# Four numbers of a recording kernel's time estimate set anew: split product, GpSimd step, two DRAM transfers

## The chip, the cores and the metric

The kernel runs on one core of a Trainium2 chip. The metric is the device time of one execution in microseconds (us). Three runs of the kernel before gave 1656.69, 1654.39 and 1648.88 us, with a median of 1654.39 us.

## The reference, cut to what matters

Two layers act on 256 tokens of width 1024. Each layer is a feed-forward block, a mixer with three branches, and a second feed-forward block, each added to the stream after a root-mean-square norm:

```python
for l in range(DEPTH):                       # DEPTH = 2
    x = x + 0.5 * swiglu(rms_norm(x, ffn1_norm[l]), ffn1_w_gate[l], ffn1_w_up[l], ffn1_w_down[l])
    x = x + hybrid_mixer(rms_norm(x, mix_norm[l]), w_in[l], ...)
    x = x + 0.5 * swiglu(rms_norm(x, ffn2_norm[l]), ffn2_w_gate[l], ffn2_w_up[l], ffn2_w_down[l])

# inside the mixer, on proj = u @ w_in:
ya = rg_lru(conv(rg_x), ...) * gelu(rg_gate)                       # branch 0
yb = softmax-weighted dilated attention, 12 heads in 3 groups      # branch 1
yc = rms_norm(chunk_gated_delta_rule(q, k, v, g, beta)) * silu(z)  # branch 2, 8 heads
y  = (gate0 * (ya @ wa) + gate1 * (yb @ wb) + gate2 * (yc @ wc)) @ w_out

# inside the delta rule: the inverse of a unit lower triangular matrix
sol = triangular_solve(a + eye(C), concat([vb, kb * exp(gam)]), lower=True, unit_diagonal=True)
```

## The kernel before, in words

**Products.** Every weight matrix is read once from DRAM, in chunks of up to 1024 columns of 128 rows (tile `raw`). A chunk is split into a high part `wh` (a copy, mostly on ScalarE) and a low part `wl` (raw minus high, on VectorE). The activations are split in the same way into pairs of tiles `s`. One step of the inner dimension is then three matmuls of 128x128 weights on 256 columns into a PSUM bank `big`: high by high, high by low, low by high. A chunk of 1024 columns holds eight steps, that is 24 such split products. There are 12144 of them in the program, and TensorE (PE) does little else: the other matmuls, into banks `sm`, belong to attention, the delta rule and the norms. Five chunks can stand converted at once (NCONV) and six raw (NRAW).

**Order.** The order of each engine's instructions is fixed when the program is written out, by a recording layer. The split products are issued one after another in a fixed sequence of jobs. All other work is written as generators ("tasks"). After each split product `pump` looks which tasks are due and lets them issue their next few instructions. A task is due when the estimated end of what it issued last has passed on the estimated clock of PE. The estimates come from `Engine._cost` (lines 327 to 368), plus a lag per engine, and `cur.t` is moved on by hand after a DMA. On the chip each engine then works through its own list in that order, and waits by semaphores: an instruction whose data is late holds up everything behind it on its engine.

**The delta rule.** Task `pair` (from line 1033) treats two heads; there are four pairs in each layer, so eight in all. Its triangular inverse goes like this. VectorE writes the diagonal 16x16 blocks to `A16` (line 1121; on the engine it reads `TENSOR_TENSOR arena<-arena 128x64`). A DMA writes them to DRAM (`rd`, line 1123), a second one reads them back, spread over all partitions, into `RR`, 1024 columns of the arena (line 1127). GpSimd (POOL) then does 30 small steps (lines 1137 to 1141), which invert the blocks, and only then is `RR` given back (line 1143). VectorE spreads the result with one multiply into `M32` (line 1149; `TENSOR_TENSOR arena<-arena,cst 128x128`), transposes it, and PE goes on with 16x16 and 32x32 products (`MATMUL sm<-arena 32x16`), then 64x64 and 128x128 ones.

**Attention.** Task `heads4` treats four heads (two slots of two). For each slot it takes twice 1152 columns of the arena, multiplies queries by keys, adds the distance term on VectorE (`SCALAR_TENSOR_TENSOR arena<-cst,sm 128x384`), takes a maximum, the exponential and the sum, scales, transposes on PE and multiplies by the values. While pairs are unfinished, tasks without an order number, such as `heads4`, may take arena space only if 3072 columns stay free (`keep`). The products of branch 1 need its results `yb`, those of branch 2 need `yc`.

The lines that the change touches are 336, 358, 1124 and 1130:

```python
336                return max(0.427 * n, 0.83 * m)
358            return (330 + 160 * n) if k.get("op") == ALU.pow else 240 + 2.2 * n
1124        self.cur.t += 2200.0
1130        self.cur.t += 2800.0
```

Of the kernel before, what the change touches and what calls it, by code (L numbers as in the profile page):

```python
# [13 lines left out]
ALU = mybir.AluOpType  # L14
# [6 lines left out]
T = 256  # L21
# [224 lines left out]


class Slots:
    """Places of T columns, each taken by one tile after another, of either type."""

    def __init__(self, pr, pool, n):
        self.pr, self.pool = pr, pool
# [52 lines left out]
def _free(ap):  # L305
    n = 1
    for x in ap.shape[1:]:
        n *= x
    return n


class Engine:
    """An engine whose instructions are counted into the estimate of the time that the order is chosen by."""

    def __init__(self, pr, key, eng):
        self._pr, self._key, self._eng = pr, key, eng
# [12 lines left out]
    def _cost(self, name, a, k):  # L329
        key = self._key  # L330
        if key == "pe":
            lhsT = k["lhsT"] if name == "matmul" else a[1]
            rhs = k["rhs"] if name == "matmul" else a[2]
            n, m = _free(rhs), _free(lhsT)
            if lhsT.dtype == F32R:
                return max(0.427 * n, 0.83 * m)
            if name == "transpose":
                return 0.84 * max(n, m)
            if m <= 32 and lhsT.shape[0] <= 32:
                return 40.0  # L340
            if m <= 64 and lhsT.shape[0] <= 64 and n <= 64:
                return 100.0
            return 1.7 * max(n, m)
        n = _free(a[0])
        if name == "tensor_reduce":
            n = _free(a[1])
        if key == "a":
            c = 93 + 0.833 * n
            for x in ("scale", "bias", "accum_out"):
                c += 93 * (not isinstance(k.get(x, 0.0), float) and x in k)  # L350
            func = a[2] if name == "activation" else None
            sets = TABLES.get(func)
            if sets and self._pr.table not in sets:
                self._pr.table = sets[0]
                c += 1283
            return c
        if key == "g":
            return (330 + 160 * n) if k.get("op") == ALU.pow else 240 + 2.2 * n
        if name == "reciprocal":
            return 68 + 6.3 * n  # L360
        fast = name in ("tensor_copy", "tensor_scalar") and a[1].space != PSUM
        c = 68 + (0.52 if fast else 1.04) * n
        if name in ("scalar_tensor_tensor", "tensor_scalar") and not isinstance(a[2], float):
            c += 60
        if k.get("accum_out") is not None:
            c += 60
        return c
# [5 lines left out]
class Prog:  # L373
# [65 lines left out]
        o += l * PRM["_n"]  # L439
        return self.prm[:, o:o + n]  # L440

# [1 line left out]
    @property  # L443
    def now(self):
        return self.clock["pe"]
# [132 lines left out]
        assert None not in out  # L578
        return out

# [1 line left out]
    def load_group(self, part=None):  # L582
        gi = self.dma_next
        self.dma_next += 1
        for key in [x for x in self.raw_t if x[0] == gi - NRAW]:
            del self.raw_t[key]
        cols = self.groups[gi][1]
        src = self.io["wts"][self.goff[gi]:self.goff[gi] + P * cols].rearrange("(p c) -> p c", p=P)
        if part is not None:
            n = cols // 2  # L590
            s = slice(part * n, part * n + n)
            self.dma_next -= 1 - part
        else:
            s = slice(0, cols)
        self.raw_t[gi, s.stop] = self.load(self.raw[gi % NRAW][:, s], src[:, s])
# [40 lines left out]
        c = next(s.stop for s in self.pieces(k) if s.stop > col)  # L636
        self.until(lambda: self.conv_t.get((k, c), 1e18) <= self.now)

# [1 line left out]
    def need(self, *key):  # L640
        self.until(lambda: self.when.get(key, 1e18) <= self.now)
        h, l = self.ops[key]
        return h.ap, l.ap
# [49 lines left out]
                    if k < total:  # L693
                        self.pump()

# [1 line left out]
    def refresh(self, j, gain, start=False):  # L697
        xj = self.X[:, j, :]
        hl = yield from self.halves()
        self.move(hl[0].ap, xj, gain[:, j:j + 1])  # L700
        yield
        self.v.scalar_tensor_tensor(hl[1].ap, xj, gain[:, j:j + 1], hl[0].ap.bitcast(F32), op0=ALU.mult, op1=ALU.subtract)
        self.mark("x", j, hl)
        if start:
            self.cur.rank = 2
            yield
        if self.nsq is None:
            self.nsq = 0
            self.a.activation(self.ssq, xj, AF.Square)
        else:  # L710
            sq = yield from self.space(T)
            self.a.activation(sq.ap, xj, AF.Square)
            yield
            self.v.tensor_tensor(self.ssq, self.ssq, sq.ap, op=ALU.add)
            sq.free()
        yield
        self.nsq += 1
# [20 lines left out]
        sq.free()  # L738
        self.norm_ready = True

# [1 line left out]
    def ffn(self, l, w, next_gain, last):  # L742
        self.norm_ready = False
        self.spawn(self.norm_chain(), 1)
        jobs = ffn_jobs(l, w)
        for kind, f, chunks in jobs[:KF]:
            b = self.big_bank()
            for i, ch in enumerate(chunks):
                self.stationary(b[:, i * T:(i + 1) * T], [ch], "x", done=f == KF - 1 and i == 1)
            self.spawn(self.gate_up(b, f), 1)  # L750
        for kind, j, chunks in jobs[KF:]:
            b = self.big_bank()
            self.stationary(b[:, :T], chunks, "h", done=j == KD - 1)
            self.spawn(self.residual(b, 0.5, j, next_gain, last), 1)
# [23 lines left out]
        else:  # L778
            yield from self.refresh(j, next_gain)

# [1 line left out]
    def move(self, dst, src, scale=None):  # L782
        """A copy, times a constant or a column, by the engine that will be through with it first."""
        n, now = _free(src), self.now
        ap = scale is not None and not isinstance(scale, float)
        ta = max(self.clock["a"], now) + 93 + 0.833 * n + 93 * ap
        tv = max(self.clock["v"], now) + 68 + (1.04 if src.space == PSUM else 0.52) * n + 60 * ap
        step = self.step
        self.step = set()
        if ta <= tv + TILT:  # L790
            self.a.activation(dst, src, AF.Copy, **({} if scale is None else {"scale": scale}))
        elif scale is None:
            self.v.tensor_copy(dst, src)
        else:
            self.v.tensor_scalar(dst, src, scale, None, op0=ALU.mult)
        self.step = step | {"m"}
# [52 lines left out]
        self.v.tensor_tensor(hl[1].ap, src, hl[0].ap.bitcast(F32), op=ALU.subtract)  # L849
        self.mark(key, k, hl)  # L850

# [1 line left out]
    def prepare(self, l):  # L853
        lam = self.p(l, "lam")
        z, = self.tinies(1, 8)
        self.v.tensor_scalar(z.ap, lam, -1.0, None, op0=ALU.mult)
        yield
        yield from self.softplus_tiny(self.rc[l][:, 0:8], z.ap, -8.0)
        yield
        self.v.tensor_scalar(self.rc[l][:, 8:16], self.rc[l][:, 0:8], -1.0, None, op0=ALU.mult)  # L860
        self.v.tensor_scalar(self.qg[l].ap, self.p(l, "qn"), 0.125, None, op0=ALU.mult)
        z.free()
        yield EXP
        self.a.activation(self.ea[l].ap, self.p(l, "alog"), AF.Exp)
        self.prepared.add(l)
# [162 lines left out]
    def pair(self, l, h0):  # L1028
# [36 lines left out]
        A, QT = yield from self.spaces([512, 1024])  # L1065
# [3 lines left out]
        for hh, h in enumerate(heads):  # L1069
# [8 lines left out]
            n = 2 * hh  # L1078
# [42 lines left out]
        self.v.tensor_tensor(a16, t4[:, :, 0, :], t4[:, :, 1, :], op=ALU.add)  # L1121
        yield
        self.nc.sync.dma_start(self.rdram[l][h0 // 2], A16.ap)
        self.cur.t += 2200.0
        yield
        src = self.rdram[l][h0 // 2].rearrange("(b k) c -> b (k c)", k=16)
        self.nc.sync.dma_start(RR.ap, src.unsqueeze(1).to_broadcast([8, 16, 1024]))
        t1.free()
        A16.free()
        self.cur.t += 2800.0  # L1130
        yield
        r4 = RR.v("p (k n j) -> p n k j", n=4, k=16)
        M16, tmp = yield from self.spaces([64, 64])
# [138 lines left out]
        for hh in range(2):  # L1272
            n = 2 * hh + 1
# [59 lines left out]
            for x in (self.beta, self.gam, self.suf):  # L1333
                x.free()

# [1 line left out]
    def att_v(self, b, g):  # L1337
        v = yield from self.space(2 * T)
        self.move(v.ap, b)
        self.big.give(b)  # L1340
        yield
        self.vt[g] = v
# [106 lines left out]
                for x in d.values():  # L1449
                    x.free()  # L1450

# [1 line left out]
    def conv_rg(self, b, l, j):  # L1453
        y = yield from self.space(T)
        w = self.p(l, "rgw")[:, 4 * j:4 * j + 4]
        s = b[:, :T]
        self.a.activation(y.ap, s, AF.Identity, scale=w[:, 3:4], bias=self.p(l, "rgb")[:, j:j + 1])
        yield
        for k in (1, 2, 3):
            self.v.scalar_tensor_tensor(y[:, k:], s[:, :T - k], w[:, 3 - k:4 - k], y[:, k:], op0=ALU.mult, op1=ALU.add)  # L1460
            if k < 3:
                yield
        self.big.give(b)
        yield
        self.xa[j] = y
# [65 lines left out]
            yield  # L1531
            self.hr[j] = self.xa[j]

# [1 line left out]
    def merge(self, b, i):  # L1535
        t = yield from self.space(T)
        self.a.activation(t.ap, b[:, :T], AF.Tanh, scale=0.5)
        self.big.give(b)
        yield
        self.tg[i] = t  # L1540
# [164 lines left out]
```

## Time and profile before

| | |
|---|---|
| median of three runs (lowest, highest) | 1654.39 us (1648.88, 1656.69) |
| profiled execution: span from first to last instruction | 1649.0 us |
| PE busy | 1611.5 us (98%) |
| VectorE (DVE) busy | 1147.7 us (70%) |
| ScalarE (ACT) busy | 932.1 us (57%) |
| GpSimd (POOL) busy | 127.3 us (8%) |
| chain that ended last | PE, products into `big` |

The page gives the span alone for the profiled execution; the lowest of the three runs, 1648.88 us, is its nearest neighbour. PE is never far from full, so what can be read off is small: where PE stands still and for whom, and where it runs at a lower granted clock. Both happen only in the two mixers, from about 300 to 550 us and from about 1100 to 1350 us. In the rows below, line L323 is the recording layer itself, through which all instructions go; the tile names tell the work apart.

### The profile page before, as it was taken

What the parts mean: (1) busy time and instruction counts of PE and PEld (TensorE: products, weight loads), DVE (VectorE), ACT (ScalarE), POOL (GpSimd) and SP (SyncE); (2) the same over time, 40 slices, a digit from 0 to 9 for tenths busy, and PEclk for the clock granted to TensorE, in tenths of its full rate; (3) what the DMA queues carried; (4) which work ended last, traced back from release to release, by engine and by line L of the source; (5) the groups of instructions that cost most, each with busy time, mean ns of one, the idle gap of its engine ahead of it and who ended that gap; (6) DMA issues with size and microseconds to landing.
All of it is one profiled execution on the core that took longest, in us unless ns stands there. A gap on an engine that the chain in (4) does not pass through costs nothing. (4 is left out here: it accounts for less than half of the span.)

```text
span 1649.0 us, 34412 instructions
## 1 busy us (share of the span) xinstructions
PE 1611.5 (98%) x13952; PEld 1569.5 (95%) x13952; DVE 1147.7 (70%) x2156; ACT 932.1 (57%) x1652; POOL 127.3 (8%) x280
## 2 busy tenths in 40 slices
PE   9999999899999999999999999998989999999999
PEld 8999999888888999999999999998989989999999
DVE  8665688777875667666566656887868746676653
ACT  6544456776855546444454445667768545464442
POOL 0000000235102000000000000002440020000000
PEclk9999999998999999999999999999999999999999
DMA  8655655444243555555655555654533435665552
GB/s 309 185 186 181 189 191 187 136 141 137 95 154 106 182 190 185 187 189 173 196 185 190 179 184 184 193 180 128 168 110 122 143 111 174 193 188 183 185 184 89
DMA packets 84943, 279.05 MB, mean 169 GB/s; under 512 B 10256, under 2 KB 15664, under 8 KB 84784
## 3 DMA queue, kind: packets, MB, share of 16 engines
q1 hardware_dynamic: 84784, 276.85, 53.6%
q8 instruction: 110, 1.80, 0.4%
q14 instruction: 49, 0.40, 0.1%
HBM read 275.49 MB, written 1.33 MB: 168 GB/s over the span
## 5 line engine op out<-in xcount | busy, mean ns | idle before, releaser
L323 PE MATMUL big<-s,wh 128*128 128x256 f32 (+1 forms) x7520 | 1354.2, 281 | 4.1 <-DVE s L323 1.9
L323 PEld LDWEIGHTS big<-s,wh 128*128 128x128 f32 (+1 forms) x7520 | 1154.8, 188 | 15.4 <-issue 6.3
L323 PE MATMUL big<-s,wl 128*128 128x256 f32 (+1 forms) x3760 | 1057.0, 281 | 0.0
L323 DVE TENSOR_TENSOR wl<-raw,wh 128x1024 fp32r<-128x1024 f32 (+3 forms) x523 | 620.1, 1186 | 292.5 <-ACT wh L323 289.0
L323 ACT ACTIVATE wh<-raw 128x1024 fp32r<-128x1024 f32 (+4 forms) x499 | 512.3, 1027 | 459.3 <-issue 252.6
L323 PEld LDWEIGHTS big<-s,wl 128*128 128x128 f32 (+1 forms) x3760 | 706.3, 188 | 2.5 <-issue 1.7
L323 PE MATMUL sm<-arena 32*32 32x32 f32 (+8 forms) x1448 | 112.7, 238 | 18.6 <-DVE arena L323 18.5
L323 POOL TENSOR_TENSOR tiny<-tiny,half 128x4 f32<-128x4 f32 (+1 forms) x28 | 42.8, 1536 | 1102.7 <-DVE tiny L323 1062.7
L323 PEld LDWEIGHTS sm<-arena 32*32 32x32 f32 (+5 forms) x1448 | 85.3, 140 | 38.0 <-DVE arena L323 14.1
L323 PE MATMUL big<-wh,s 128*128 128x256 f32 x576 | 112.0, 292 | 0.0
L323 ACT ACTIVATE s<-s 128x256 fp32r<-128x256 f32 (+1 forms) x216 | 85.3, 407 | 21.4 <-DVE s L323 21.1
L323 PEld LDWEIGHTS big<-wh,s 128*128 128x128 f32 x576 | 92.7, 196 | 0.8
L323 POOL TENSOR_TENSOR arena<-arena 128x60 f32<-128x60 f32 (+14 forms) x240 | 81.5, 340 | 121.4 <-DMA arena<-rd 103.5
L323 PE MATMUL big<-wl,s 128*128 128x256 f32 x288 | 85.1, 295 | 0.0
L323 DVE SCALAR_TENSOR_TENSOR s<-big,prm,s 128x255 f32<-128x255 f32 (+2 forms) x171 | 79.4, 476 | 7.4 <-ACT s L323 5.7
L323 DVE TENSOR_TENSOR s<-s,s 128x256 fp32r<-128x256 f32 (+1 forms) x185 | 77.1, 422 | 3.2 <-ACT s L323 2.7
L323 DVE TENSOR_TENSOR arena<-big,zr 128x512 f32<-128x512 f32 x88 | 60.7, 691 | 24.5 <-PE big L323 24.5
L323 ACT ACTIVATE arena<-sm 128x128 f32<-128x128 f32 (+6 forms) x155 | 49.0, 317 | 49.8 <-PE sm L323 47.0
L323 ACT ACT_TABLE_LOAD x56 | 71.8, 1283 | 1.6 <-PEq L1697 0.7
L323 PEld LDWEIGHTS big<-wl,s 128*128 128x128 f32 x288 | 56.6, 196 | 0.5
L323 ACT ACTIVATE s<-big,prm 128x256 f32<-128x256 f32 x53 | 26.5, 501 | 50.0 <-PE big L323 50.0
L323 ACT ACTIVATE s<-big 128x256 f32<-128x256 f32 x54 | 20.6, 381 | 59.4 <-PE big L323 59.4
(108 smaller groups left out, 770.2 us busy)
## 6 DMA issues: line engine op xcount, KB each, us to landing
raw<-wts SPq DMA_DIRECT2D x435, 512.0 KB, 3.7
raw<-wts SPq DMA_DIRECT2D x64, 448.0 KB, 3.7
raw<-wts SPq DMA_DIRECT2D x16, 384.0 KB, 2.9
arena<-rd SPq DMA_DIRECT2D x8, 512.0 KB
arena<-rgw SPq DMA_DIRECT2D x4, 512.0 KB, 5.6
arena<-gd SPq DMA_DIRECT2D x16, 128.0 KB, 4.1
X<-x SPq DMA_DIRECT2D x4, 256.0 KB, 4.3
raw<-wts SPq DMA_DIRECT2D x4, 256.0 KB, 3.6
```

Of the source, the lines that this page charges most:

```text
L323: r = f(*a, **k)
```

## The change

Four numbers of the estimate are set anew. Nothing else in the program is changed but comments; every instruction is the same, and only the order in which the engines' lists are written can differ. A split product is estimated at 0.46 ns per column of its 256 (it was 0.427). A GpSimd step that isn't a power is estimated at 350 + 0.6 n ns for n columns (it was 240 + 2.2 n). After the write of `A16` to DRAM the task waits 5500 ns (it was 2200), and after the read into `RR` 8500 ns (it was 2800).

```diff
             if lhsT.dtype == F32R:
-                return max(0.427 * n, 0.83 * m)
+                return max(0.46 * n, 0.83 * m)
...
         if key == "g":
-            return (330 + 160 * n) if k.get("op") == ALU.pow else 240 + 2.2 * n
+            return (330 + 160 * n) if k.get("op") == ALU.pow else 350 + 0.6 * n
...
         self.nc.sync.dma_start(self.rdram[l][h0 // 2], A16.ap)
-        self.cur.t += 2200.0
+        self.cur.t += 5500.0
...
-        self.cur.t += 2800.0
+        self.cur.t += 8500.0
```

What this does to the lists is seen at three places. The first is VectorE's list in the first mixer, at the first pair of heads: the rows from `A16` (the first) to `M32` (the last), of what lies between only the low parts of weight chunks. Before:

```order
L323 TENSOR_TENSOR arena<-arena 128x64
...
L323 TENSOR_TENSOR wl_78<-raw_70,wh_73 128x1024
...
L323 TENSOR_TENSOR wl_79<-raw_71,wh_74 128x1024
...
L323 TENSOR_TENSOR wl_80<-raw_72,wh_75 128x1024
...
L323 TENSOR_TENSOR wl_81<-raw_67,wh_76 128x1024
...
L323 TENSOR_TENSOR wl_82<-raw_68,wh_77 128x1024
...
L323 TENSOR_TENSOR wl_78<-raw_69,wh_73 128x1024
L323 TENSOR_TENSOR arena<-arena,cst 128x128
```

And in the changed kernel, the same stretch of VectorE's list:

```order
L323 TENSOR_TENSOR arena<-arena 128x64
...
L323 TENSOR_TENSOR wl_78<-raw_70,wh_73 128x1024
...
L323 TENSOR_TENSOR wl_79<-raw_71,wh_74 128x1024
...
L323 TENSOR_TENSOR wl_80<-raw_72,wh_75 128x1024
...
L323 TENSOR_TENSOR wl_81<-raw_67,wh_76 128x1024
...
L323 TENSOR_TENSOR wl_82<-raw_68,wh_77 128x1024
...
L323 TENSOR_TENSOR wl_78<-raw_69,wh_73 128x1024
...
L323 TENSOR_TENSOR wl_79<-raw_70,wh_74 128x1024
...
L323 TENSOR_TENSOR wl_80<-raw_71,wh_75 128x1024
...
L323 TENSOR_TENSOR arena<-arena,cst 128x128
```

`M32` stood six chunks behind `A16` and stands eight behind it now. Over the eight pairs of the program the chunks between the two were 6, 4, 4, 5, 5, 7, 5 and 5 (41), and are 8, 8, 7, 9, 8, 7, 7 and 8 (62).

The second place is VectorE's list in the first mixer at the last pair. `arena<-arena,cst 128x128` is `M32` again, and `arena<-cst,sm 128x384` is the last attention slot adding its distance term. Before:

```order
L323 TENSOR_TENSOR wl_79<-raw_68,wh_74 128x1024
L323 SCALAR_TENSOR_TENSOR arena<-cst,sm_97 128x384
L323 SCALAR_TENSOR_TENSOR arena<-cst,sm_94 128x384
L323 SCALAR_TENSOR_TENSOR arena<-cst,sm_95 128x384
L323 TENSOR_REDUCE tiny<-arena 128x1 x2
L323 TENSOR_TENSOR wl_80<-raw_69,wh_75 128x768
L323 TENSOR_TENSOR arena<-arena,cst 128x128
L323 STREAM_TRANSPOSE arena<-arena 128x128
```

And in the changed kernel:

```order
L323 TENSOR_TENSOR wl_78<-raw_72,wh_73 128x1024
L323 TENSOR_TENSOR wl_79<-raw_67,wh_74 128x768
L323 TENSOR_TENSOR arena<-arena,cst 128x128
L323 STREAM_TRANSPOSE arena<-arena 128x128
L323 SCALAR_TENSOR_TENSOR arena<-cst,sm_93 128x384
L323 SCALAR_TENSOR_TENSOR arena<-cst,sm_96 128x384
L323 SCALAR_TENSOR_TENSOR arena<-cst,sm_93 128x384
L323 TENSOR_REDUCE tiny<-arena 128x1
```

The last attention slot stood ahead of `M32`, with weight chunks in between, and stands behind it now.

The third place is PE's list at the same point. `sm` rows with `128x128` and `128x256` are the slot's queries by keys, those with `32x16` and `32x32` the pair's inverse; `big` rows are split products. Before, the slot's queries by keys stood like this:

```order
L323 MATMUL sm_97<-arena 128x128
L323 MATMUL sm_97<-arena 128x256
L323 MATMUL big_92<-s_2453,wh_75 128x256
L323 MATMUL big_92<-s_2454,wh_75 128x256
L323 MATMUL sm_94<-arena 128x128
L323 MATMUL sm_94<-arena 128x256
L323 MATMUL big_92<-s_2453,wl_80 128x256
L323 MATMUL big_92<-s_2482,wh_75 128x256
L323 MATMUL sm_95<-arena 128x128
L323 MATMUL sm_95<-arena 128x256
```

And in the changed kernel:

```order
L323 MATMUL big_91<-s_5700,wl_80 128x256
L323 MATMUL sm_93<-arena 128x128
L323 MATMUL sm_93<-arena 128x256
L323 MATMUL sm_96<-arena 128x128
L323 MATMUL sm_96<-arena 128x256
L323 MATMUL sm_95<-arena 32x16 x16
L323 MATMUL sm_93<-arena 128x128
L323 MATMUL sm_93<-arena 128x256
L323 MATMUL sm_96<-arena 32x16 x16
L323 MATMUL sm_95<-arena 32x32 x8
L323 MATMUL sm_93<-arena 32x32 x12
```

The small products stood among split products. Now 92 of them, of the slot and of the pair, follow each other without a split product between; the next split product needs the slot's result `yb`.

## Rows read from the trace of the kernel before

**Rows 1.** The page: busy time, share of the span and instructions of each engine.

```profile
PE 1611.5 (98%) x13952; PEld 1569.5 (95%) x13952; DVE 1147.7 (70%) x2156; ACT 932.1 (57%) x1652; POOL 127.3 (8%) x280
```

**Rows 2.** Waits, whole span: who waited for whom, total us, times, longest us.

```profile
PE sm L323 <- DVE arena L323: 27.2, 9, 4.7
...
PE big L323 <- DVE s L323: 1.9, 4, 0.8
...
DVE arena L323 <- POOL arena L323: 26.5, 8, 6.6
```

**Rows 3.** Windows of 50 us: busy us (instructions) PE PEld DVE ACT POOL; clock, DMA.

```profile
300.00:350.00 50.00, 45.04 (x450) 42.81 (x449) 39.80 (x101) 37.77 (x74) 12.36 (x33) 0.97 0.51 154
350.00:400.00 50.00, 45.83 (x422) 42.35 (x421) 34.72 (x109) 33.45 (x84) 21.91 (x41) 0.90 0.46 128
400.00:450.00 50.00, 47.13 (x465) 44.40 (x465) 41.71 (x102) 42.36 (x103) 14.71 (x30) 0.97 0.30 96
...
550.00:600.00 50.00, 50.00 (x427) 50.00 (x426) 31.71 (x45) 24.00 (x34) 0.00 (x0) 1.00 0.62 199
...
1100.00:1150.00 50.00, 44.87 (x387) 42.15 (x385) 38.46 (x115) 35.78 (x66) 10.57 (x32) 0.93 0.47 133
...
1200.00:1250.00 50.00, 45.44 (x477) 42.04 (x476) 33.58 (x84) 34.41 (x100) 16.29 (x35) 0.93 0.35 106
...
1300.00:1350.00 50.00, 46.73 (x443) 42.27 (x443) 27.78 (x56) 21.83 (x45) 10.83 (x32) 0.97 0.34 102
```

**Rows 4.** Timeline, first pair, first mixer: start us, us, engine, work, [idle before <- releaser].

```profile
299.81 0.21 DVE L323 TENSOR_TENSOR arena<-arena 128x64 f32<-128x64 f32 x1
...
302.00 0.42 SPq L1123 DMA_DIRECT2D rd<-arena  x1
...
305.64 0.70 SPq L1127 DMA_DIRECT2D arena<-rd  x1
...
313.51 11.96 POOL L323 TENSOR_TENSOR arena<-arena 128x60 f32<-128x60 f32 x30 [19.61 <-DMA arena<-rd]
...
325.50 0.29 DVE L323 TENSOR_TENSOR arena<-arena,cst 128x128 f32<-128x128 f32 x1 [6.04 <-POOL arena L323]
...
326.58 0.44 PE L323 MATMUL sm<-arena 32*32 32x16 f32 x32 [4.36 <-DVE arena L323]
```

**Rows 5.** Timeline of VectorE, last pair of the first mixer: `A16` and `M32`.

```profile
493.08 0.22 DVE L323 TENSOR_TENSOR arena<-arena 128x64 f32<-128x64 f32 x1
...
515.61 0.29 DVE L323 TENSOR_TENSOR arena<-arena,cst 128x128 f32<-128x128 f32 x1 [3.09 <-POOL arena L323]
```

**Rows 6.** Short windows, columns as in rows 3.

```profile
378.00:380.00 2.00, 2.00 (x33) 1.87 (x25) 1.60 (x3) 0.00 (x0) 1.06 (x1) 0.50 0.80 238
...
516.00:518.00 2.00, 1.70 (x43) 1.67 (x44) 1.97 (x6) 0.22 (x1) 0.00 (x0) 1.00 0.03 8
...
1175.60:1194.70 19.10, 17.97 (x153) 17.67 (x153) 16.44 (x48) 14.50 (x33) 16.79 (x33) 1.00 0.49 167
```

**Rows 7.** Groups of instructions by form: count, busy us, mean ns, idle before.

```profile
L323 DVE TENSOR_TENSOR wl<-raw,wh 128x1024 fp32r<-128x1024 f32 x433 | 529.4, 1223 | 245.8 <-ACT wh L323 242.4
...
L323 DVE SCALAR_TENSOR_TENSOR arena<-cst,sm 128x384 f32<-128x384 f32 x24 | 13.2, 551 | 14.6 <-PE sm L323 14.6
...
L323 ACT ACTIVATE arena<-sm 128x384 f32<-128x384 f32 x24 | 11.7, 488 | 11.6 <-PE sm L323 11.3
...
L323 DVE TENSOR_REDUCE tiny<-arena 128x1 f32<-128x768 f32 x8 | 7.5, 943 | 0.0
...
L323 ACT ACTIVATE arena<-arena,tiny 128x768 f32<-128x768 f32 x8 | 7.4, 923 | 0.0
...
L323 DVE TENSOR_SCALAR arena<-arena,tiny 128x768 f32<-128x768 f32 x8 | 5.9, 742 | 0.0
```

**Rows 8.** Timeline of PE: attention's weights by values, then queries by keys.

```profile
503.59 2.18 PE L323 MATMUL sm<-arena 128*64 128x128 f32 x18
506.13 0.92 PE L323 MATMUL sm<-arena 64*128 64x128 f32 x4
```

## The prediction

> **What bounds the kernel now.** I read the page first, then the waits, the windows, and the timeline of one pair. The page shows PE busy for 1611.5 of 1649.0 us [rows 1]. A stretch of plain split products shows PE full at granted clock 1.00, with 427 products in 50 us, which is 117.1 ns each [rows 3]. The number of products doesn't change, so only what PE loses beside them can be won. The waits show one large loss: PE waited 27.2 us, 9 times, for VectorE's arena tiles, and VectorE waited 26.5 us, 8 times, for POOL [rows 2]; there are eight pairs of heads. The timeline of the first pair shows that the two are one chain. `A16` is ready at 300.02, the write to DRAM is issued at 302.00, the read at 305.64, POOL starts at 313.51 and works for 11.96 us, `M32` starts at 325.50 after VectorE had stood still for 6.04 us, and PE goes on at 326.58 after 4.36 us without work [rows 4]. VectorE works its list in order, so behind the waiting `M32` stand the splits and the pieces that PE wants next.
>
> The windows show a second loss. In the six windows with such stops the granted clock was 0.97, 0.90, 0.97, 0.93, 0.93 and 0.97; in plain stretches it is 1.00 [rows 3]. The lower level is 0.50 (1.2 instead of 2.4 GHz), and PE can be busy all the time at it [rows 6]. What it cost is the missing share times 50 us: 1.5 + 5.0 + 1.5 + 3.5 + 3.5 + 1.5 = 16.5 us. Together the stops and what follows them are worth 27.2 + 16.5 = 43.7 us, 2.6% of the span.
>
> **The change, part by part.** *Split product, 0.427 to 0.46.* For 256 columns the estimate goes from 109.3 to 117.8 ns; the trace has 117.1 [rows 3]. PE's clock ran 7% too fast in the estimate, and now it doesn't. In the feed-forward blocks PE is already full [rows 3], so I take 0 there.
>
> *The two transfers.* From `A16` to POOL's start the trace has 313.51 − 300.02 = 13.5 us [rows 4]. The old waits were 2.2 + 2.8 = 5.0 us, the new ones are 14.0.
>
> *GpSimd step.* The 30 steps of a pair have 4 to 60 columns, 32 in the mean. The old estimate is 30 × 310 ns = 9.3 us, the new one 30 × 369 ns = 11.1 us; the trace has 11.96 [rows 4].
>
> From `A16` to `M32` that makes 14.3 us before and 25.1 us now, against 325.50 − 300.02 = 25.5 us in the trace of this pair and 515.61 − 493.30 = 22.3 us in that of the last pair [rows 4, 5]. `M32` stood too early in VectorE's list. The order shows it moved: over the eight pairs 62 weight chunks stand between `A16` and `M32` instead of 41. Each chunk is 24 split products of 117.1 ns, 2.8 us of PE's time. So 21 more chunks are 59 us, 7.4 us a pair, where the stops were 27.2 / 8 = 3.4 us a pair and 4.7 at most [rows 2]. I take it that all the stops of this kind go and with them the low clock: −43.7 us. What is late next is no longer this chain but VectorE's own pace (below). The move takes the read into `RR` past weight loads in SP's queue. Between the two transfers stand one or two loads, as before none to two. A load held behind the read is wanted up to five converted chunks later, 14 us, so I take 0 for it.
>
> *What the later `M32` drags along.* `RR` is held until POOL is through, and attention's last slot in the first mixer needs arena space. It stood before `M32` and stands behind it now. On PE its products and the pair's now follow each other, 92 small ones, and the next split product needs the slot's result. So here PE must live through the slot's chain. Queries by keys take 3 × 0.92 = 2.8 us [rows 8], the last distance step 0.55, the two reductions 0.94 and (my estimate for the half as wide one, 0.6 of it) 0.57, the exponentials 0.92 and 0.55, the scaling 0.74 and 0.45 [rows 7], three copies out of PSUM 3 × 0.49 and about 0.5 for the transposes, weights by values 2.18 [rows 8], and the split of the result about 0.8 (two passes of 256 columns, estimated from 1.22 for 1024). That is 12.5 us, and 13 with the handovers. Queries by keys and weights by values are 5.0 of it on PE; the pair's own products in the hole are at most another 5. This work was there before and isn't extra, so 3 to 8 us of standing still remain. To these comes a late start. Nine chunks (198 products, 23.2 us) now lie between `A16` and the hole, and the chain needs 22.3 to 25.5 us, so 0 to 2.3 us. The further tiles of the slot follow one by one, about 1 us. The low clock behind a stop comes on top, 2 to 5 us by the windows [rows 3]. The hole costs between 6 and 16 us; I take 10, near the middle, since both ends are made of the same rows.
>
> *What nothing hides any more.* PE's estimate was 7% short, and so is VectorE's: a low part of 1024 columns is estimated at 68 + 1.04 × 1024 = 1133 ns and takes 1223 [rows 7], 8% more. Before, both errors cancelled; now PE's is right and VectorE's is not. In the mixers each result that PE awaits can come a little late. The lower bound is 0, as VectorE stands idle for 6 to 22 us in every 50 [rows 3]. A gain is excluded, since nothing of VectorE's work goes. The upper bound is 8% of about 500 us of mixer, 40 us. I take 9, nearer to 0, because even in its fullest window VectorE is busy for only 41.7 of 50 us [rows 3].
>
> The sum against the profiled execution: −43.7 + 10 + 9 = −24.7, or 1649.0 to 1624.3 us. The median of the runs is 5.4 us above that span, so I forecast 1624.3 + 5.4 = 1629.7, about 1630 us. Its own range is 1619 (hole and lateness at 6 and 2) to 1642 (16 and 15).
>
> **The rivals.** *Half the stops stay.* The chain itself may grow. POOL's 30 steps took 11.96 us while VectorE stood still for half of them [rows 4]. In a stretch where VectorE was busy for 16.44 of 19.10 us POOL was busy for 16.79 with three steps more [rows 6], and VectorE will now work through. For it also speaks that one pair has no more chunks in between than before (7 and 7). Against it stands the mean of 7.4 us more where 3.4 were missing. With half of 43.7 kept, the hole at 12 and lateness at 6, the sum is −21.9 + 18 = −3.9, and the time 1650.5: no change. The Trainium skill, "SBUF — State Buffer", section "Who interferes with whom", speaks for this rival: a VectorE instruction with two SBUF inputs and a GpSimd instruction that reads SBUF exclude each other through a shared port, and the later one waits for the whole of the other. The row of the busy stretch leans its way; by the rule each low part (1.22 us) that gets in first would put off a POOL step by that much.
>
> *VectorE becomes the bound (slower).* If the 8% show in full, VectorE's list trails PE's through both mixers: +40 us of waits, and since the stops would be as many as the old ones, their 16.5 us of low clock come back. With the hole that is −43.7 + 40 + 16.5 + 10 = +22.8, or 1677 us. It decides from 42 us of new cost beside the hole (43.7 − 10 + 8.3). For it speaks that VectorE has only 8.3 of 50 us free in its fullest window [rows 3]; against it, that 8% of the 41.7 us there are 3.3, and so still find room.
>
> *The hole is hidden.* If the slot's chain runs beside POOL after all, only 5 us are lost: −43.7 + 5 = −38.7, and 1616 us. The list order of PE speaks against it.
>
> **How the numbers follow.** The forecast has 0.55, half the stops 0.19, the slower case 0.11, the hidden hole 0.15. Changes under 0.5% (8.3 us) can't be told from none here. Faster by more than that: 0.55 + 0.15 = 0.70. Within: 0.19. Slower: 0.11. The range goes from 1613, a little below the hidden hole, to 1656, past the case with half the stops; it leaves the slower case out.
>
> **What would show it.** VectorE's wait for POOL should fall from 26.5 us to under 5, and PE's for VectorE's arena tiles with it, but for the hole; the windows of the pairs should be back at clock 1.00. About 24 us behind the last `A16` of the first mixer PE should show its longest stop, of some 4 to 11 us in pieces, with the clock low behind it; in the second mixer there should be none like it. If VectorE still waits for POOL, the chain was mis-sized. If PE waits in many small pieces for VectorE and ScalarE, the 8% were what counted. The forecast is wrong if the low clock stays although the stops go, or if the new stop is beyond 16 us.

## The result, and the profile after

The changed kernel takes 1627.02 us (median of 4 runs, 1625.22 to 1630.48), against 1653.31 us for the kernel before on the same chip (4 runs, 1648.88 to 1656.69). The ratio is 0.9846, with a 95% interval of 0.9826 to 0.9865. The forecast was 1630 us. The profiled execution, the one whose trace is shown below, has a span of 1625.4 us where before had 1649.0, so 23.6 us less; its own time was 1627.63 us.

The page's first part, columns as in [rows 1]:

```profile
PE 1602.4 (99%) x13952; PEld 1560.0 (96%) x13952; DVE 1159.2 (71%) x2172; ACT 936.7 (58%) x1643; POOL 139.3 (9%) x280
```

PE does the same 13952 products in 9.1 us less of busy time. It stands still for 1625.4 − 1602.4 = 23.0 us, where it was 1649.0 − 1611.5 = 37.5. The waits say which stops went (waiting engine, released by, total us, times, longest us), to be held against [rows 2]:

```profile
PE sm L323 <- DVE arena L323: 8.6, 8, 2.2
...
PE big L323 <- DVE s L323: 6.0, 10, 2.3
...
DVE arena L323 <- POOL arena L323: 1.8, 3, 0.7
```

VectorE's wait for POOL fell from 26.5 to 1.8 us. PE's wait for VectorE's arena tiles fell with it from 27.2 to 8.6 us, and its wait for split inputs grew from 1.9 to 6.0. The windows of 50 us, columns as in [rows 3], show where the rest is:

```profile
300.00:350.00 50.00, 50.00 (x495) 46.94 (x494) 46.84 (x134) 42.23 (x82) 18.64 (x38) 1.00 0.54 170
350.00:400.00 50.00, 47.75 (x475) 45.50 (x475) 37.74 (x102) 41.51 (x105) 31.99 (x63) 0.97 0.42 129
400.00:450.00 50.00, 47.65 (x475) 44.02 (x474) 43.34 (x100) 40.30 (x91) 3.65 (x3) 1.00 0.42 136
...
500.00:550.00 50.00, 45.83 (x427) 42.04 (x426) 25.33 (x50) 24.39 (x63) 8.63 (x21) 0.86 0.33 102
1100.00:1150.00 50.00, 49.41 (x491) 46.96 (x490) 45.20 (x118) 44.69 (x80) 14.08 (x32) 1.00 0.58 173
...
1200.00:1250.00 50.00, 45.89 (x464) 42.87 (x464) 44.07 (x103) 41.33 (x100) 6.94 (x12) 1.00 0.41 127
...
1300.00:1350.00 50.00, 50.00 (x515) 48.64 (x515) 28.06 (x51) 28.14 (x69) 9.21 (x23) 1.00 0.45 142
```

The first pair's window (300 to 350) is full at clock 1.00; it had 4.96 us without PE and clock 0.97. One window of the first mixer is worse than before: 500 to 550, with 4.17 us without PE and clock 0.86. The last window of the second mixer, its counterpart, is full.

Summed over eleven windows (300 to 550 and 1050 to 1350 us, the two mixers), PE stands still for 15.0 us (29.7 before) and the low clock costs 8.5 us (16.5 before; the missing share times 50 us, as in the prediction). Together that is 22.7 of the 23.6 us.

The timeline of the first pair after the change, to be held against [rows 4] (start us, us, engine, work, [idle before <- releaser]):

```profile
297.78 0.22 DVE L323 TENSOR_TENSOR arena<-arena 128x64 f32<-128x64 f32 x1
...
311.50 10.82 POOL L323 TENSOR_TENSOR arena<-arena 128x60 f32<-128x60 f32 x24 [13.14 <-DMA arena<-rd]
322.28 1.46 POOL L323 TENSOR_TENSOR tiny<-tiny,half 128x4 f32<-128x4 f32 x1
323.71 2.95 POOL L323 TENSOR_TENSOR arena<-arena 128x12 f32<-128x12 f32 x6
...
327.29 0.28 DVE L323 TENSOR_TENSOR arena<-arena,cst 128x128 f32<-128x128 f32 x1
```

The two transfers still take as long: from the end of `A16` at 298.00 to POOL's start 13.5 us. POOL ends at 326.66, and VectorE comes to `M32` at 327.29. The row has no bracket: nothing is waited for. The cover, that is the work between `A16` and `M32` in VectorE's list, is enough by 0.6 us.

It is not enough everywhere. At five of the eight pairs VectorE still comes to `M32` before POOL is through, but only by 0.1 to 0.7 us. The second pair:

```profile
364.37 0.29 DVE L323 TENSOR_TENSOR arena<-arena,cst 128x128 f32<-128x128 f32 x1 [0.48 <-POOL arena L323]
```

The chain itself grew. Summed over the eight pairs, the time from the end of `A16` to POOL's last step was 207 us before and is 239 us now, so 32 us more: 14 before POOL's first step and 18 from there on.

Behind the last pair's `M32` in the first mixer comes the new stop. The same view there, from its `A16`, with PE's rows behind:

```profile
481.88 0.23 DVE L323 TENSOR_TENSOR arena<-arena 128x64 f32<-128x64 f32 x1
...
495.15 13.96 POOL L323 TENSOR_TENSOR arena<-arena 128x60 f32<-128x60 f32 x30 [7.73 <-DMA arena<-rd]
...
507.18 1.57 PE L323 MATMUL sm<-arena 64*128 64x128 f32 x8
...
508.08 0.96 DVE L323 TENSOR_TENSOR wl<-raw,wh 128x768 fp32r<-128x768 f32 x1 [1.77 <-ACT wh L323]
...
509.14 0.29 DVE L323 TENSOR_TENSOR arena<-arena,cst 128x128 f32<-128x128 f32 x1
...
509.83 2.46 PE L323 MATMUL sm<-arena 32*32 32x16 f32 x68 [1.08 <-DVE arena L323]
513.10 0.64 PE L323 MATMUL sm<-arena 32*32 32x32 f32 x16 [0.81 <-DVE arena L323]
515.18 0.93 PE L323 MATMUL sm<-arena 32*32 32x32 f32 x24 [1.44 <-DVE tiny L323]
...
520.57 3.91 PE L323 MATMUL sm<-arena 128*64 128x128 f32 x18
...
529.01 1.16 PE L323 MATMUL sm<-arena 128*128 128x128 f32 x8 [0.69 <-ACT arena L323]
```

Here the cover is just used up: VectorE is free at 508.08 + 0.96 = 509.04, POOL ends at 495.15 + 13.96 = 509.11, and `M32` starts at 509.14. From 507.18 to 525.26 PE has no split product at all; these 18 us are the 92 small products of the list (the trace has 167 rows for them). The stops shown in brackets are short, 0.69 to 1.44 us, and make 4.0 us. The row with 3.91 us shows the other half of the price: the same 18 products took 2.18 us in [rows 8]. Short windows tell why:

```profile
508.00:510.00 2.00, 0.92 (x24) 0.52 (x26) 1.78 (x4) 0.05 (x1) 1.03 (x2) 1.00 0.51 201
...
512.00:514.00 2.00, 0.93 (x40) 0.69 (x32) 1.97 (x5) 0.77 (x3) 0.00 (x0) 0.50 0.00 0
...
520.00:522.00 2.00, 2.00 (x13) 1.88 (x13) 0.00 (x0) 0.50 (x2) 0.00 (x0) 0.50 0.00 0
...
524.00:526.00 2.00, 2.00 (x18) 1.83 (x17) 0.27 (x1) 0.46 (x2) 0.00 (x0) 0.96 0.00 0
```

The granted clock is 0.50 (1.2 GHz) from about 511 to 524, for most of that with PE busy. The hole, as I call this stretch, costs 4.17 + 0.14 × 50 = 11.2 us.

### The profile page after: what moved, and what is told of

Same layout as the page of the kernel before. It is cut to its first block, busy times and chain, and to the rows that moved or that the text cites. A ratio compares the mean times of both kernels' runs of the same rounds, so it can differ in the third digit from the quotient of the medians.

```text
span 1625.4 us, 34428 instructions
## 1 busy us (share of the span) xinstructions
PE 1602.4 (99%) x13952; PEld 1560.0 (96%) x13952; DVE 1159.2 (71%) x2172; ACT 936.7 (58%) x1643; POOL 139.3 (9%) x280
## 5 line engine op out<-in xcount | busy, mean ns | idle before, releaser
L323 POOL TENSOR_TENSOR tiny<-tiny,half 128x4 f32<-128x4 f32 (+1 forms) x28 | 38.6, 1378 | 1102.0 <-DVE tiny L323 1083.9
L323 PE MATMUL sm<-arena 128*128 128x128 f32 (+7 forms) x1440 | 114.0, 238 | 9.7 <-DVE arena L323 6.9
L323 POOL TENSOR_TENSOR arena<-arena 128x60 f32<-128x60 f32 (+14 forms) x240 | 98.6, 411 | 62.6 <-DMA arena<-rd 44.7
L323 DVE SCALAR_TENSOR_TENSOR s<-big,prm,s 128x255 f32<-128x255 f32 (+2 forms) x183 | 85.6, 477 | 6.6 <-ACT s L323 5.3
L323 ACT ACTIVATE s<-big 128x256 f32<-128x256 f32 x53 | 20.2, 382 | 62.1 <-PE big L323 62.1
L323 ACT ACTIVATE s<-big,prm 128x256 f32<-128x256 f32 x53 | 26.5, 499 | 45.2 <-PE big L323 45.0
```

The lines of the kernel that those rows point to most:

```text
L323: r = f(*a, **k)
```

## The experiments

The set-off texts are what was expected, written down before each run. Theory A is the prediction's: the two transfer waits move `M32` behind POOL's end, that is the gain, and the hole and small late results give part of it back. Its main rival here, B, holds that the gain is PE's own pace in the estimate (0.46), which makes all hand-offs fit. The other letters stand for single questions and are told at their runs. Each kernel ran on the same chip as the kernel before, and the ratio is to that.

The table gathers the profiled executions. "Chunks" are the weight chunks between `A16` and `M32` in VectorE's list, summed over eight pairs; "run" is the longest sequence of small products in PE's list without a split product between; "PE still" is the span less PE's busy time; "low clock" is the missing share of the granted clock times 50 us, summed over all windows of 50 us. The last three columns are in us and from the profiled execution.

| kernel | chunks | run | ratio (95% interval) | span | PE still | low clock |
|---|---|---|---|---|---|---|
| before | 41 | 25 | 1 | 1649.0 | 37.5 | 17.5 |
| the change | 62 | 92 | 0.9846 (0.9826, 0.9865) | 1625.4 | 23.0 | 10.5 |
| e5, the change again | 62 | 92 | 0.9878 (0.9856, 0.9900) | 1631.3 | 24.0 | 12.0 |
| e1, transfers alone | 57 | 22 | 0.9876 (0.9835, 0.9917) | 1630.3 | 17.3 | 13.5 |
| e2, split product alone | 38 | 25 | 1.0153 (1.0119, 1.0188) | 1668.8 | 55.4 | 20.0 |
| e9, GpSimd step alone | 45 | 92 | 1.0012 (0.9997, 1.0027) | 1652.7 | 42.9 | 27.0 |
| e3, change without transfers | 41 | 40 | 1.0130 (1.0093, 1.0167) | 1660.9 | 48.4 | 24.0 |
| e8, change without GpSimd step | 58 | 20 | 0.9854 (0.9828, 0.9879) | 1623.8 | 22.4 | 6.5 |
| e4, less reserve | 60 | 20 | 0.9821 (0.9791, 0.9851) | 1616.6 | 16.6 | 3.0 |
| e6, less reserve again | 60 | 20 | 0.9789 (0.9765, 0.9814) | 1616.5 | 17.7 | 1.0 |
| e10, less reserve, longer wait | 66 | 18 | 0.9816 (0.9796, 0.9835) | 1616.5 | 18.1 | 4.0 |
| e11, less reserve, gate wait | 61 | 20 | 0.9833 (0.9817, 0.9849) | 1620.0 | 20.2 | 4.0 |
| e7, less reserve, VectorE × 1.08 | 62 | 20 | 0.9937 (0.9915, 0.9959) | 1634.5 | 27.9 | 10.5 |
| e12, as e7, gate wait | 61 | 20 | 0.9810 (0.9795, 0.9825) | 1616.4 | 14.8 | 5.0 |

The same kernel run on two chips differs in its ratio by 0.003 (the change and e5, e4 and e6). Smaller differences between runs on different chips carry nothing.

### Which of the four numbers

**e1, the two transfers alone**, in the kernel before:

```diff
-        self.cur.t += 2200.0
+        self.cur.t += 5500.0
...
-        self.cur.t += 2800.0
+        self.cur.t += 8500.0
```

> Only the two waits after the DRAM transfers are set anew (5500 and 8500); the split product stays at 0.427 and the GpSimd step at 240 + 2.2 n. In the lists 57 weight chunks stand between A16 and M32 over the eight pairs (41 before, 62 in the change), and the longest run of small products without a split product is 22 (25 before, 92 in the change). Theory A, that the gain is VectorE no longer waiting for POOL at M32: VectorE's wait for POOL under 4 us (26.5 before), the stops and the low clock go, there is no hole of 92 products, so it is faster than the change itself: 1612 to 1622 us. Rival B, that the gain comes from the right pace of PE (0.46): the stops stay in half or more, 1640 us or above.

Measured: 1629.28 us (1622.11 to 1633.36). The mechanism holds (VectorE's wait for POOL is 4.2 us, a little over the 4 expected), but A's time was too low. The waits, columns as above:

```profile
DVE arena L323 <- POOL arena L323: 4.2, 5, 1.3
...
PE sm L323 <- DVE arena L323: 2.2, 2, 1.2
```

The chain's waits are all but gone, and PE stands still less than in the change itself. Most of what is missing against A's time went, in the profiled execution (1632.34 us), to the low clock of one window, 8.5 us, with hardly a stop in it (last section). Of the other three executions one was as long, at 1633.36 us and a mean granted clock of 0.991; the two with 0.995 and 0.998 took 1626.22 and 1622.11 us.

**e2, the split product alone**, in the kernel before:

```diff
-                return max(0.427 * n, 0.83 * m)
+                return max(0.46 * n, 0.83 * m)
```

> Only the split product is set anew (0.46); the transfers stay at 2200 and 2800 and the GpSimd step at 240 + 2.2 n. 38 chunks stand between A16 and M32 (41 before). Theory A: VectorE's wait for POOL stays at 25 to 35 us, PE's wait for VectorE's arena tiles at 25 us or more, and the time is 1650 to 1662 us. Rival B: most of the change's gain is here, 1625 to 1638 us.

Measured: 1673.77 us (1670.79 to 1678.43), 1.5% slower than before. B is refuted; A has the direction and is too low by more than 10 us. The waits:

```profile
DVE arena L323 <- POOL arena L323: 35.5, 8, 6.9
PE sm L323 <- DVE arena L323: 27.3, 8, 6.2
...
PE sm L323 <- DVE tiny L323: 9.2, 2, 5.7
```

With PE's pace right and the transfers still 5.0 us, `M32` comes even earlier (38 chunks), and VectorE waits 35.5 us for POOL, where it was 26.5. One reading is that PE's too fast clock had stretched the list of the kernel before and so hidden part of the too short waits. That isn't shown: PE's wait for VectorE's arena tiles is as before (27.2), and what PE lost in addition are other waits, above all the 9.2 us for `tiny` tiles.

**e3, the change without the transfers** (2200 and 2800 put back):

```diff
-        self.cur.t += 5500.0
+        self.cur.t += 2200.0
...
-        self.cur.t += 8500.0
+        self.cur.t += 2800.0
```

> The change with the two transfer waits undone (2200 and 2800); split product and GpSimd step as in the change. 41 chunks stand between A16 and M32, as before; two runs of 40 small products without a split product are in PE's list. Theory A: as before the change within 0.5%, 1647 to 1662 us, with VectorE's wait for POOL at 20 us or more. Rival B: 1625 to 1638 us.

Measured: 1669.36 us (1663.16 to 1672.43). B is refuted here too, and A's range was again too low. VectorE's wait for POOL is that of before, and PE waits more:

```profile
PE sm L323 <- DVE arena L323: 33.1, 9, 6.2
...
DVE arena L323 <- POOL arena L323: 26.1, 6, 6.9
```

This list has as many chunks between `A16` and `M32` as the one before (41), and is 1.3% slower all the same. So fewer chunks can't be the whole reason why the new split product loses without the transfers; the rest of the reason is open.

**e8, the change without the GpSimd step**, and **e9, the step alone** in the kernel before (the same line, in the other direction):

```diff
-            return (330 + 160 * n) if k.get("op") == ALU.pow else 350 + 0.6 * n
+            return (330 + 160 * n) if k.get("op") == ALU.pow else 240 + 2.2 * n
```

> The change with the GpSimd step undone (240 + 2.2 n); split product and transfers as in the change. 58 chunks between A16 and M32 (62 in the change), longest run of small products 20, so the hole is gone as in e6 though the reserve is 3072. If the step's number mattered for the chain, VectorE's wait for POOL would come back (over 6 us) and the time be above e5; if it does nothing but shift the lists, VectorE's wait for POOL stays under 5 us and the time is that of e6 within 5 us.

> Only the GpSimd step is set anew (350 + 0.6 n). 45 chunks stand between A16 and M32 (41 before), and PE's list holds a run of 92 small products without a split product, in the second mixer. Theory A: four more chunks are 11 us of cover, so VectorE's wait for POOL falls from 26.5 to 15 to 22 us, and the hole gives back about as much: 1643 to 1658 us. Rival: the step's number is a good part of the change's gain, 1640 us or less.

Measured for e8: 1627.44 us (1626.16 to 1630.65), ratio 0.9854 against 0.9878 for the change (e5) on the same chip. VectorE's wait for POOL is 4.6 us, under 5 as expected. The time is 9 us over e6 and was expected within 5 of it: a miss. In the traces e8 has 4.7 us more of PE standing still and 5.5 us more of low clock than e6. Among the stops are two single waits that e6 hasn't, 2.7 us of small products for a `tiny` tile and 1.5 for the recurrent gate's weights; which item of the order brings them was not found.

Measured for e9: 1653.74 us (1647.44 to 1657.62), no change, as A expected. Its trace still says something. The step moved `M32` a little (45 chunks), and the waits fell a little, VectorE's for POOL less than the expected 15 to 22 us:

```profile
DVE arena L323 <- POOL arena L323: 23.6, 7, 5.7
...
PE sm L323 <- DVE arena L323: 18.3, 6, 5.7
```

That is 8.9 us less of PE's wait than before. But its list also has a run of 92 small products, this time in the second mixer, and the window there paid for it:

```profile
1300.00:1350.00 50.00, 42.09 (x393) 37.40 (x390) 26.89 (x61) 18.42 (x40) 11.19 (x32) 0.86 0.38 107
```

In [rows 3] the same stretch had 46.73 us of PE at 0.97: the new one loses (46.73 − 42.09) + 0.11 × 50 = 10.1 us more. The stop at `M32` itself, 5.7 us in its timeline, is in it, since this list still has `M32` too early; before, that stop took 3.3 us. So the run of 92 can come without the longer transfers, and what it costs there apart from the stop is not separated. Of the lists with the new step and the old reserve two have a run of 92 (the change and e9) and one has two runs of 40 (e3); none of the lists with the old step is above 25.

So of the four numbers the two transfers make the gain, the step by itself changes the time by nothing that can be measured, and the split product loses by itself.

### The hole

The hole was put down to arena space: the last attention slot can't start while a pair holds its tiles and the reserve for further pairs is kept free. **e4** and **e6** are the change with less reserve:

```diff
-KEEP, KEEP2 = 3072, 2048
+KEEP, KEEP2 = 2048, 2048
```

`KEEP` is the number of arena columns that a task without an order number, such as attention, must leave free while pairs are unfinished.

> The change, with the reserve of arena columns that attention has to leave free cut from 3072 to 2048 (KEEP). The run of 92 small products is gone from PE's list (longest 20), 60 chunks between A16 and M32. Theory A, that the hole is made by attention waiting for the columns that RR holds and costs some 11 us (4.2 us of standing still and 7 us of low clock between 500 and 550 us in the change's trace): 1612 to 1620 us, clock 1.00 in that stretch. Rival C, that the slot's chain is late in any case and PE only waits at another place: within 0.3% of the change, 1622 to 1632 us, with PE's waits as many.

> The changed kernel itself, beside the next three on one chip, so that they are compared with it and not only with the kernel before. Both theories: 0.982 to 0.987 of the time before.

> The change with the reserve KEEP at 2048, as in e4_less_reserve, once more beside the change. If the hole of 92 small products costs what the change's trace shows between 500 and 550 us (4.2 us of standing still, 7 us of low clock, of which PE's own small products there would take a little anyway), this is 7 to 12 us faster than e5_change_again. If PE would only have waited elsewhere, under 3 us.

Measured: e4 1619.10 us (1617.80 to 1621.37); on another chip e5, the change again, 1631.99 (1630.10 to 1633.52) and e6 1618.52 (1611.97 to 1619.53). A's time for e4 was met. e5's ratio lies just above what was expected, and e6 is 13.5 us under it, a little more than the 7 to 12 expected; in the traces the hole's window makes 11.0 us of that. The run of 92 is gone from the list, and the window with it (e6):

```profile
500.00:550.00 50.00, 50.00 (x517) 48.94 (x516) 29.36 (x52) 27.38 (x64) 1.01 (x1) 1.00 0.48 151
```

PE is full at clock 1.00 where the change had lost 11.2 us. The waits of the pairs stayed away: VectorE's for POOL is 1.3 us. So the smaller reserve is shown to remove the hole. It is not the only thing that does: with the old step and the old reserve (e8) the run of 92 is gone too. e4 and e6 are 1.8 to 2.1% under the kernel before; no other version is clearly faster. What the reserve is worth without the four numbers was not tried.

### More cover, and VectorE's estimate

All four remaining kernels have the small reserve. **e10** makes the second wait longer:

```diff
-        self.cur.t += 8500.0
+        self.cur.t += 11500.0
```

> As e6 (the change, reserve 2048), with 11500 instead of 8500 after the read into RR. 66 chunks between A16 and M32 (60 in e6), longest run of small products 18. Theory A: the cover was already enough, since VectorE's wait for POOL was 1.3 us in e6, so more of it wins nothing: within 0.4% of e6, 1613 to 1626 us. Rival D, that more distance always helps: below 1612 us.

Measured: 1619.58 us (1618.12 to 1625.65), ratio 0.9816, no different from e4's 0.9821, as theory A expected. From 41 to some 60 chunks the waits for POOL vanish; 66 win nothing more.

**e7** puts VectorE's estimate up by the 8% that the prediction said it was short:

```diff
+        scale = 1.08 if key in "v" else 1.0
...
-            pr.count(key, self._cost(name, a, k))
+            pr.count(key, scale * self._cost(name, a, k))
```

> As e6, and VectorE's estimates are 8% larger (the measured 1223 ns against the estimated 1133 for a low part). 62 chunks between A16 and M32, longest run of small products 20, so neither of the two large causes moves. Theory L, that results of VectorE coming 8% later than estimated cost the change some 9 us of PE's waits: 4 to 9 us faster than e6, with PE's waits for VectorE down from some 12 us to 5 or less. Rival N, that these waits come from the list order of single tasks and not from the scale of the estimate: within 3 us of e6.

Measured: 1641.78 us (1636.44 to 1642.39), 23 us slower than e6. Both theories are refuted. The trace names a new wait. VectorE, then PE (lines are one higher in this kernel):

```profile
449.58 0.61 DVE L324 SCALAR_TENSOR_TENSOR arena<-arena,tiny,cst 128x128 f32<-128x128 f32 x2 [2.26 <-DMA arena<-gd]
...
456.56 1.65 PE L324 MATMUL sm<-arena 64*128 64x128 f32 x4 [4.27 <-DVE arena L324]
```

VectorE waits 2.26 us for the read of the pair's decay sums (`gd`), up to 449.58; from 452.3 to 456.56 PE stands still for an arena tile that VectorE writes after that. The low clock follows, and the window loses (50 − 43.97) + 0.10 × 50 = 11.0 us, where e6 loses nothing:

```profile
450.00:500.00 50.00, 43.97 (x292) 37.30 (x293) 37.18 (x102) 30.84 (x55) 6.33 (x13) 0.90 0.29 86
```

Over the whole span VectorE waits 13.6 us for `gd`, 5.9 in e6.

That read has a wait of its own in the estimate, 3500 ns. **e11** sets it higher with the small reserve alone, **e12** with VectorE's 8% as well:

```diff
-        self.cur.t += 3500.0
+        self.cur.t += 6500.0
```

> As e6, with 6500 instead of 3500 after the read of the decay sums (arena<-gd), a third wait set by hand. VectorE waited for this transfer for 5.9 us, 7 times, in e6, and 10.9 us in the change. Theory G, that this is the next wait of the same kind: VectorE's wait for it under 2 us and 2 to 5 us faster than e6. Rival N, that it is hidden behind PE's work: within 2 us of e6.

> As e7 (reserve 2048, VectorE's estimates 8% larger), with 6500 instead of 3500 after the read of the decay sums. In e7 VectorE waited for that transfer for 13.6 us, and behind one such wait (2.26 us) the attention's piece came late and PE stood for 4.27 us with the low clock behind it. Theory G, that e7 lost its 23 us by such single waits and not by its scale: the stop between 450 and 500 us goes and the time is 1612 to 1625 us. Rival S, that the larger scale itself spoils the order: 1632 us or more.

Measured: e11 1623.55 us (1622.03 to 1625.25), ratio 0.9833: VectorE's wait for `gd` is gone from its trace, but there is no gain, against theory G; with e4 and e6 at 0.9821 and 0.9789, a loss of a few us isn't excluded. VectorE's wait for POOL is back at 7.1 us there. e12 1620.04 us (1618.47 to 1620.79), ratio 0.9810: the loss of e7 is gone, as theory G expected, and the window from 450 to 500 us is full at 1.00. So e7's loss goes when this read is given more time. The sum of the waits for `gd` doesn't set it, since e10 has 14.1 us of them without a loss; it is the place where one of them falls, and 11.0 of the 23 us lie at such a place. The 8%, with that loss taken out, win nothing over the small reserve alone.

## Why the prediction came out right

**The stops at `M32`** (−43.7 us) were the main term, and e1 and e3 show both sides of it: with the two transfers alone the waits go, without them they stay and the time is over that of before. The sign to look for was VectorE's wait for POOL under 5 us; it is 1.8. That it was enough was luck, though. By the prediction the 21 chunks were 59 us against 27.2 us of stops, so 32 us to spare; the chain grew by just these 32 us. The windows of the pairs are at 1.00 but for two: one at 0.97, and the hole's.

**The hole** was forecast at 10 us (6 to 16), in pieces, behind the last `A16` of the first mixer and nowhere in the second; it is 11.2 us, begins 26.9 us after that `A16` (508.75 − 481.88) where about 24 were forecast, and the second mixer has none. The standing still is at the low end and the low clock longer than thought: 4.2 us, where I had 4 to 11 in pieces, and 7.0 us, where I had 2 to 5. The two differences nearly cancel. The cause given, space, holds in so far as e4 and e6 remove the hole by it. It was too narrow in naming `RR`: e8 holds `RR` through the same two transfers and has no run of 92, and e9 has one without the longer waits. The new GpSimd step belongs to it.

**The lateness** (+9 us) came out near in size, but not by its reason. In the mixers the change loses 15.0 + 8.5 = 23.5 us, without the hole 12.3. Before lost 29.7 − 27.2 = 2.5 us besides the stops, so 9.8 us are new. The reason was VectorE's estimate being 8% short; the row on which it rests is still there (1224 ns for a low part in the changed kernel). But scaling it up lost 23 us in e7 and, with the gate read mended, won nothing in e12. The small waits are therefore not shown to come from that 8%; they hang on single places of the order, as e7, e8 and e11 move them about, and what sets them is open. That 9 us came out near 9.8 is luck. (The size was also read from too few rows: the fullest window of the mixers before had VectorE busy for 43.5 us, from 1250 to 1300, and not for 41.7.)

**The sum**, −24.7 us on the span, met −23.6. Its first two parts are right in their cause, the third is right in size for a reason that the runs don't bear out. From span to median I had added 5.4 us; here it is 1627.02 − 1625.4 = 1.6, and the profiled execution's own time lies 2.2 us above its span.

**The rivals.** *Half the stops stay* had its mechanism right: the chain did grow, and POOL did get slower once VectorE worked through. The 30 steps of the first pair took 10.82 + 2.95 = 13.8 us, where [rows 4] has 11.96 with VectorE standing still for half of them. The Trainium skill, "SBUF — State Buffer", section "Who interferes with whom", says that a GpSimd instruction that reads SBUF and a VectorE instruction with two SBUF inputs lock each other out of a shared port; the longer steps agree with it, though no run here separates that from other causes. The longer chain cost no more than waits of 0.1 to 0.7 us, because the 21 further chunks just covered it. *VectorE becomes the bound* did not come: in its fullest window VectorE is busy for 46.8 of 50 us, and PE is full there. *The hole is hidden* is what e4 and e6 make of the change: 1619 us, where 1616 was worked out.

What the prediction didn't look into is how much a single right number can lose. It took 0 for the split product in the feed-forward blocks and gave it no term of its own in the mixers; e2 shows +23 us (1673.77 against 1650.93) when it stands alone. With the new transfers nothing of that can be seen: e1 without it (0.9876) and e8 with it (0.9854) can't be told apart.

## What to carry to other kernels

Where a table of estimates sets the order of in-order engines, compare each hand-set wait with the trace from producer to consumer: here 5.0 us stood for 13.5, and an engine's consumer placed too early stopped not only its own engine but the next one, and then cost low clock too. A number that is set right can lose while others are still wrong (e2), so try the numbers together and singly. After moving a consumer, measure its chain anew: here the chain grew by as much as the move had to spare. When a longer wait holds memory longer, look for who asks for that memory next: here 13.5 us hung on a reserve of 1024 columns.

## What the runs showed of the hardware

The low clock does not follow the length of a stop. In e1 PE stood still for 1.17 us only, among small products, and some 2 us later the clock went to 0.50 and stayed there for some 17 us while PE was busy throughout. The timeline's row and the short windows of e1, columns as above:

```profile
413.60 0.44 PE L323 MATMUL sm<-arena 32*32 32x16 f32 x32 [1.17 <-DVE arena L323]
```

```profile
412.00:414.00 2.00, 0.83 (x37) 0.61 (x36) 2.00 (x7) 1.44 (x5) 0.00 (x0) 1.00 0.02 6
...
416.00:418.00 2.00, 2.00 (x7) 1.34 (x6) 1.73 (x6) 0.93 (x3) 0.00 (x0) 0.53 0.60 178
...
424.00:426.00 2.00, 2.00 (x9) 1.56 (x7) 1.53 (x2) 0.00 (x0) 0.00 (x0) 0.50 0.00 0
```

The low clock behind that one stop cost 8.5 us (0.83 in its window of 50 us). In the changed kernel the window from 1200 to 1250 has 4.1 us without PE and clock 1.00 throughout. Nor does the list alone set it: e1's four executions have mean granted clocks of 0.992, 0.991, 0.998 and 0.995, and the two higher ones are 6 to 11 us shorter. What tells the cases apart, the kind of products or their place, was not tried.
